# Row copies in place of small transfers for rotated attention queries, and new delays, in a two-layer hybrid trunk

## The chip, the cores and the metric

The kernel runs on one core of one Trainium2 chip. Its time is the device time of one execution in microseconds, as the median of several runs. TensorE (PE in the profile), VectorE (DVE), ScalarE (ACT), GpSimd (POOL) and SyncE (SP) each work through an instruction queue of their own; transfers are issued from the queues of SyncE and ScalarE.

## The reference

The program computes two layers over 1024 tokens of 1024 features. Cut to what the change touches:

```python
def hybrid_layer(x, ...):
    mod = c_act @ w_mod + b_mod                     # shift, scale, gate
    h = rms_norm(x, pre_gain) * (1.0 + scale) + shift
    proj = h @ w_in                                 # columns for three head groups
    aq = apply_rotary(aq.reshape(B, S, ATTN_HEADS, HEAD_DIM), positions, rope_freq)
    ak = apply_rotary(ak.reshape(B, S, ATTN_KV_HEADS, HEAD_DIM), positions, rope_freq)
    a_out = sliding_window_attention(aq, ak, av, sinks) * jax.nn.silu(ag)
    ...
    y = jnp.concatenate([a_out, r_out, g_out], axis=-1) @ w_out
    return x + gate * rms_norm(y, post_gain)

def apply_rotary(x, positions, inv_freq):
    ...
    x1, x2 = jnp.split(x.astype(jnp.float32), 2, axis=-1)
    out = jnp.concatenate([x1 * cos - x2 * sin, x2 * cos + x1 * sin], axis=-1)
```

The attention has 8 query heads of 64 features over 2 key heads, a window of 128 tokens and one learned sink per head. Retention and gated linear attention have 4 heads each and run in chunks.

## The kernel before, in words

Tokens lie in 8 tiles of 128. Weights and activations are split into a high and a low part (`fp32r`, a rounding copy, and the residue), and each product is made in three passes. So each projected tile needs two small jobs per half of its features: a rounding copy on ScalarE (L650) and a subtraction for the residue (L651). The entries `hlo0` and `hlo1` of the table `EN` name the engine of the residue of the first and the second half: GpSimd (G) and VectorE (V). They are used for tiles 2 to 7 of layer 0 and all 8 of layer 1, 14 each. L624 scales a tile by its norm before TensorE transposes it (L176) into PSUM. Weights stream through buffers `st`, are rounded by L145 on ScalarE or L147 on VectorE, and their residues made by L497 on VectorE or GpSimd into `arena`; the output weights are scaled as well (L486, L487).

PSUM has 8 banks: 3 under the name `mm` for the large products, 5 under `aux` for everything else.

The order of TensorE's work is made by a planner in the kernel's text: it keeps a clock of the work issued (`clk`), a list of jobs (generators) and flags. A job yields a delay or a flag to wait for; at points between the wide products (`pump`) the planner runs the jobs that are due. The delays stand in the table `L`, looked up by `lat(key, layer)`; a key with `@1` is for layer 1. The order on the other engines follows from that order and a scheduler's model. No delay is waited for on the chip; they only place the work in the queues.

The attention of a layer goes so. `attn_kv` rotates the keys of a tile on VectorE (`rotary`, L842 to L848), transposes them on TensorE and splits them into `kT` (L858, L859). `attn_rot` is called four times per layer, for the two halves of the tokens (`hf`) and the two head groups (`g`). It loads cosine and sine from `tabS`, makes the projected queries transposed, 128 features by 512 tokens, in two products, and rotates them on VectorE: L890 and L891 multiply, L893 and L894 add. The result in `u[0]`, `u[1]` has its halves of 32 rows in the wrong partitions. So L897 copies `u[j]` to `q[j]` on ScalarE, and four transfers (the entry `qst`, on SyncE, issued in the helper `dma` at L150) then move 32 rows of 512 numbers each, 64 KB, from `u` to other partitions of `q`. After the delay `aq6` a job splits `q` into `mx` (L858 on ScalarE, L859 on VectorE) and sets the flag on which the scores wait, later by `aq2`.

`attn_run` goes through blocks of two tiles: `attn_scores` makes the scores of a tile in 12 small products, into two aux banks; `attn_turn` copies the previous key tile's half (L145, `smx<-aux`, on ScalarE) and the masked half (L957, VectorE), takes the maximum (L959), exponentials (L962), reciprocal (L965) and scales (L966, GpSimd), and after the delay `aq3` transposes the probabilities on TensorE (L176) into an aux bank each, which ScalarE copies out (L145, `t<-aux`). `attn_values` multiplies them by the values (`va`, `vd`) into one more aux bank, copied out by L145 as well.

In the retention part, L1407 loads the values of a chunk back from `vS` (entry `lv`, on SyncE); L1435 makes the gates of the gated linear attention after the chunks that `GGC` names. At the start, `mod_first` makes the first modulation rows, with pieces of the angle tables between its steps (`TAB_N`), and finishes the first half at the step `FIN`.

Of the kernel before, what the change touches and what calls it, by code (L numbers as in the profile page):

```python
# [13 lines left out]
AF = mybir.ActivationFunctionType  # L14
# [5 lines left out]
S = 1024  # L20
# [69 lines left out]
def trunk(ctx: ExitStack, tc: tile.TileContext, ins, cst, out):  # L90
    nc = tc.nc
    V, A, G, T = nc.vector, nc.scalar, nc.gpsimd, nc.tensor
# [16 lines left out]
    def t2(dt=F32):  # L109
        return gp.tile([P, 512], dt, tag="t2", name=nm("t2"), bufs=B2)  # L110
# [13 lines left out]
    def aux(dt=F32):  # L124
        return ps.tile([P, 512], dt, tag="aux", name=nm("aux"), bufs=8 - MMB)
# [14 lines left out]
    def eng(k):  # L140
        return G if EN[k] == "G" else V

    def copy(k, dst, src):
        if EN[k] == "A":
            A.activation(dst, src, AF.Copy)  # L145
        else:
            V.tensor_copy(dst, src)  # L147

    def dma(k, dst, src):
        {"S": nc.sync, "A": A, "P": G}[EN[k]].dma_start(dst, src)  # L150

# [138 lines left out]
    def mod_first(rws, between):  # L290
# [20 lines left out]
        for hh in range(2):  # L311
# [9 lines left out]
            for k in range(KT):  # L321
# [151 lines left out]
    def load(l, name, first=None, kcs=range(KT // 2)):  # L473
# [6 lines left out]
        for kc in kcs:  # L480
# [16 lines left out]
            i = (G if first == 0 and kc in LOG else V if first == 0 else eng(f"wlo{kc}")).tensor_tensor(wt[:, 1, 2 * kc:2 * kc + 2, 0:256], st, f(hi), ALU.subtract)  # L497
            if EN[f"wlo{kc}"] == "G" and first is None:
                after[3] = i
# [106 lines left out]
    def pre(l, t, xt, early=False, soon=False):  # L606
# [9 lines left out]
        with ExitStack() as es:  # L616
# [3 lines left out]
            for j in range(2):  # L620
                if EN[f"xn{j}"] == "A" or early and XA[t][j] == "A" or soon and XA[t][j] == "A":
                    A.activation(xn[j], xt[j], AF.Copy, scale=r)
                else:
                    scaled[t] = V.tensor_scalar(xn[j], xt[j], r, None, ALU.mult)  # L624
        yield 0.5 if early else L["pf1"] if soon else lat("pre1", l)
        if early:
# [252 lines left out]
    def attn_rot(l, hf, g, w_):  # L879


        sn, cs = t2(), t2()
        for s, d in ((0, sn), (1, cs)):
            nc.sync.dma_start(d.rearrange("p (s n) -> p s n", s=2),
                              tabS[2 * hf:2 * hf + 2, :, s, :].rearrange("s p n -> p s n"))
        u, w = [t2(), t2()], [t2(), t2()]
        for c in range(2):
            pm = mm()
            project_T(pm, l, hf, w_, c * P)
            V.tensor_tensor(u[c], pm, cs, ALU.mult)  # L890
            V.tensor_tensor(w[1 - c], pm, sn, ALU.mult)  # L891
            pump()
        V.tensor_tensor(u[0], u[0], w[0], ALU.subtract)  # L893
        V.tensor_tensor(u[1], u[1], w[1], ALU.add)  # L894
        q = w
        for j in range(2):
            A.activation(q[j], u[j], AF.Copy)  # L897
            for r in range(2):
                dst, src = 64 * r + 32 * (1 - j), 64 * r + 32 * j
                dma("qst", q[j][dst:dst + 32], u[1 - j][src:src + 32])  # L900
        mq = mix_tile().rearrange("p a k q -> p (a k q)").rearrange("p (a j n) -> p a j n", a=2, j=2)
        kv[(hf, g)] = mq
        job(split_later(mq, q, ("q", l, hf, g)))
# [438 lines left out]
    def layer(l):  # L1342
# [58 lines left out]
        for p in range(NP_):  # L1401
# [170 lines left out]
B2 = 14  # L1572
B1 = 7
BS, BST, MMB, SMB = 11, 5, 3, 6
EN = {"qst": "S", "smh": "S", "sml": "S", "sm0": "S", "sm1": "S", "lao": "S", "sao": "S", "lmix": "S", "ssg": "S", "lsg": "S", "ssr": "S", "lsr": "A", "lx": "S", "sx": "A", "lw": "S", "lwm": "S", "whi0": "V", "whi1": "A", "whi2": "A", "whi3": "A", "wlo0": "V", "wlo1": "G", "wlo2": "V", "wlo3": "G", "xn0": "V", "xn1": "V", "hlo0": "G", "hlo1": "V", "rot0": "V", "rot1": "V", "rdec": "V", "kslo": "V", "qslo": "V", "vlo": "G", "kT": "A", "qT": "A", "sprev": "A", "pn": "G", "pf0": "A", "aoc": "A", "hng": "V", "mh": "A", "gso": "V", "mg": "V", "mgl": "V", "rT": "A", "rv": "A", "sqh": "A", "sql": "V", "lv": "S", "gv": "A", "gk": "A", "ak0": "V", "ak1": "V", "ak2": "V", "ak3": "V", "kd0": "G", "kd1": "G", "kd2": "G", "kx1": "G", "kx2": "G", "kx3": "V", "kx4": "V", "qb": "G", "stx": "V"}
TURN = ("AV", "AV")
L = {"tt1": 5.86, "tt2": 6.96, "tb1": 28.02, "tb2": 0.32, "pf3": 12.26, "pf1": 6.83, "pf2": 2.88, "mod1": 3.75, "mod2": 2.4, "mod3": 17.58, "mod4": 0.05, "mod5": 0.09, "mod6": 0.05, "pre1": 7.76, "kv1": 15.26, "kv2": 2.17, "aq1": 11.36, "aq7": 4.15, "ag1": 5.72, "aq2": 2.4, "aq6": 7.35, "aq3": 11.38, "aq4": 7.65, "aq5": 2.86, "hn1": 3.34, "hn2": 10.04, "gz1": 9.1, "gz2": 13.49, "gl1": 5.15, "gd3": 15.95, "gc1": 1.82, "gc2": 1.95, "gc3": 0.62, "gc4": 4.49, "gc6": 3.2, "gc5": 4.23, "rc1": 6.33, "rc2": 0.05, "rc3": 1.29, "rc4": 3.27, "fin1": 10.23, "lay1": 0.05, "mod2@1": 2.23, "mod3@1": 15.08, "mod5@1": 2.83, "mod6@1": 3.24, "pre1@1": 10.18, "kv1@1": 4.51, "kv2@1": 0.16, "aq1@1": 6.55, "aq7@1": 7.39, "ag1@1": 8.25, "aq2@1": 2.07, "aq6@1": 9.39, "aq3@1": 11.41, "aq4@1": 6.32, "aq5@1": 1.56, "hn1@1": 4.35, "hn2@1": 9.0, "gz1@1": 6.11, "gz2@1": 8.89, "gl1@1": 20.55, "gd3@1": 15.63, "gc1@1": 2.47, "gc2@1": 4.67, "gc3@1": 0.84, "gc4@1": 0.84, "gc6@1": 1.3, "gc5@1": 0.05, "rc1@1": 5.87, "rc2@1": 2.37, "rc3@1": 2.6, "rc4@1": 5.99, "fin1@1": 6.8, "lay1@1": 0.15, "gc7": 1.43, "gc7@1": 0.05, "tb0": 0.91, "mod7": 1.05, "mod7@1": 1.25}
CHUNK = 7
VDB = 8
VDF = 6  # L1580
TAB_N = (0, 2, 2, 2, 1, 1, 2, 1, 0, 0, 1, 1, 0, 0, 0, 1)
BEGIN = 7
MIXP = (6, 7)
# [47 lines left out]
```

## Time and profile before

| | |
|---|---|
| median of 3 runs | 974.1 us (971.63 to 975.36) |
| profiled execution | 973.24 us |
| its span, first to last instruction | 971.5 us |
| mean granted clock of TensorE | 0.996 |
| TensorE busy | 941.4 us, 97% |
| VectorE busy | 629.3 us, 65% |
| ScalarE busy | 468.0 us, 48% |
| GpSimd busy | 240.5 us, 25% |

The profile is of one execution. The difference between its time and its span, 1.74 us, lies around the first and last instructions. A group of instructions is named by its line, its engine, its operation, and "out<-in" by the names of tiles. A timeline row gives start, duration, engine, line and, in brackets, the idle time before it and whom it waited for. PEld is TensorE's loading of weights, beside its products. The issue of a transfer on an engine's queue (SPq, ACTq) is timed apart from its landing.

### The profile page before, as it was taken

To read this page: it belongs to the slowest core of one execution; us is meant where nothing else is said; L and a number is where in the kernel's file an instruction comes from. 1 tells how busy PE (TensorE), PEld (TensorE's weight loads), DVE (VectorE), ACT (ScalarE), POOL (GpSimd) and SP (SyncE) were. 2 spreads that over 40 slices of the span, in tenths; PEclk is the share of its full clock that TensorE was granted. 3 is DMA by queue.
4 is the path that set the end of the run, shared out by engine and by line. 5 is a ranking of instruction groups with operands and counts; after the bars stand their busy time and mean duration, and the time that the engine had idled before them with its cause. 6 is when DMAs were issued, how large, how long until landed. Compare 5 with 4: busy or idle time off the path is not lost.

```text
span 971.5 us, 15977 instructions
## 1 busy us (share of the span) xinstructions
PE 941.4 (97%) x5645; PEld 769.3 (79%) x5645; DVE 629.3 (65%) x1334; ACT 468.0 (48%) x1149; POOL 240.5 (25%) x302
## 2 busy tenths in 40 slices
PE   5999999999999899999999999999999999999997
PEld 1699888788887677778889888887887777777886
DVE  6876847757785677764677484694667586862332
ACT  2676233454764646623455431434666566761111
POOL 3343001413230324421233110042223033440000
PEclk9999999999999999999999999999999999999999
DMA  9943425513362345687555251262133243555851
GB/s 314 317 133 119 158 72 157 179 34 117 101 199 87 111 141 179 191 273 246 174 173 182 88 180 38 91 195 66 55 99 109 66 131 99 163 174 173 281 218 65
DMA packets 126188, 144.36 MB, mean 149 GB/s; under 512 B 12078, under 2 KB 95896, under 8 KB 126108
## 3 DMA queue, kind: packets, MB, share of 16 engines
q1 hardware_dynamic: 118236, 131.63, 43.8%
q10 hardware_dynamic: 7872, 11.72, 3.4%
q8 instruction: 44, 0.72, 0.3%
q14 instruction: 36, 0.29, 0.1%
HBM read 104.51 MB, written 36.70 MB: 145 GB/s over the span
## 4 chain that ended last, share of the span: by engine, by line
PE 77%; DMA 7%; DVE 5%; ACT 5%; issue 3%; POOL 1%; SPq 0%; ACTq 0%; DVEq 0%; POOLq 0%
PE mm L161 61%; PE aux L161 13%; PE aux L176 3%; DMA st<-in_w_in_dram 1%; DVE arena L497 1%; DMA mx<-mixS 1%; DMA st<-in_w_mod_dram 1%; DMA mixS<-t 1%; DMA t<-t 1%; ACT t L145 1%; DMA xk<-in_x_dram 1%; DMA t<-in_x_dram 1%; DVE t L624 1%; DMA t<-xs 1%; ACT L1016 1%
## 5 line engine op out<-in xcount | busy, mean ns | idle before, releaser
L161 PE MATMUL mm<-arena,arena 128*128 128x512 f32 (+2 forms) x1512 | 314.2, 361 | 0.0
L161 PE MATMUL mm<-arena 128*128 128x512 f32 (+2 forms) x1392 | 286.5, 360 | 0.3 <-ACT arena L698 0.2
L161 PEld LDWEIGHTS mm<-arena,arena 128*128 128x128 f32 x1512 | 246.4, 189 | 43.0 <-issue 2.3
L161 PEld LDWEIGHTS mm<-arena 128*128 128x128 f32 x1392 | 227.6, 189 | 39.3 <-issue 2.0
L161 PE MATMUL mm<-arena,mx 128*128 128x512 f32 (+1 forms) x696 | 158.3, 386 | 0.2 <-DMA mx<-mixS 0.2
L161 PEld LDWEIGHTS mm<-arena,mx 128*128 128x128 f32 x696 | 126.5, 188 | 27.8 <-issue 1.5
L497 POOL TENSOR_TENSOR arena<-st,arena 128x512 fp32r<-128x512 f32 x57 | 84.2, 1484 | 139.2 <-ACT arena L145 80.4
L145 ACT ACTIVATE t<-aux 128x512 f32<-128x512 f32 x64 | 36.8, 590 | 77.4 <-PE aux L176 40.0
L497 DVE TENSOR_TENSOR arena<-st,arena 128x512 fp32r<-128x512 f32 x63 | 65.1, 1048 | 8.5 <-ACT arena L145 5.7
L145 ACT ACTIVATE arena<-st 128x512 fp32r<-128x512 f32 x82 | 48.1, 623 | 42.5 <-PE mm L161 28.4
L1276 ACT ACTIVATE t<-mm 128x512 f32<-128x512 f32 x30 | 18.0, 599 | 95.2 <-PE mm L161 47.8
L962 ACT ACTIVATE smx<-smx,sm 128x129 f32<-128x129 f32 x128 | 50.1, 393 | 20.9 <-DVE sm L959 20.0
L966 POOL TENSOR_TENSOR smx<-smx,sm 128x512 f32<-128x512 f32 x32 | 35.7, 1116 | 90.5 <-DVE sm L965 87.3
L373 DVE SCALAR_TENSOR_TENSOR acc<-st,c_act,acc 128x512 f32<-128x512 f32 x60 | 48.7, 812 | 6.8 <-DMA st<-in_w_mod_dram 6.0
L1277 DVE TENSOR_TENSOR t<-mm,modg 128x512 f32<-128x512 f32 x30 | 20.6, 688 | 43.4 <-ACT t L1276 43.2
L1321 DVE SCALAR_TENSOR_TENSOR t<-t,sm,t 128x512 f32<-128x512 f32 x32 | 25.0, 812 | 34.3 <-DMA t<-xs 18.2
L551 POOL TENSOR_TENSOR sm<-sm,mhalf 128x1 f32<-128x1 f32 x26 | 14.8, 570 | 111.6 <-DVE sm L550 108.7
L176 PE MATMUL aux<-c_ident,t 128*128 128x128 f32 x224 | 33.8, 274 | 6.4 <-DVE t L624 2.7
L176 PEld LDWEIGHTS aux<-c_ident,t 128*128 128x128 f32 x224 | 26.7, 141 | 12.8 <-DVE t L624 3.2
L957 DVE COPY_PREDICATED smx<-c_curmask,aux 128x256 f32<-128x256 int32 x64 | 25.7, 446 | 14.9 <-ACT smx L145 13.7
L359 POOL MEMSET acc<- 128x512 f32 x4 | 2.1, 529 | 124.1 <-PE aux L161 111.3
L1018 DVE TENSOR_TENSOR t<-t,t 128x512 f32<-128x512 f32 x16 | 11.1, 691 | 33.1 <-ACT t L1017 33.1
(223 smaller groups left out, 1349.0 us busy)
## 6 DMA issues: line engine op xcount, KB each, us to landing
st<-in_w_in_dram SPq DMA_DIRECT2D x96, 256.0 KB, 3.2
st<-in_w_mod_dram SPq DMA_DIRECT2D x64, 256.0 KB, 3.7
mixS<-t SPq DMA_DIRECT2D x64, 256.0 KB, 2.6
mx<-mixS SPq DMA_DIRECT2D x28, 512.0 KB, 5.1
st<-in_w_out_dram SPq DMA_DIRECT2D x32, 256.0 KB, 3.2
wm<-in_w_mod_dram SPq DMA_DIRECT2D x12, 512.0 KB, 5.7
t<-in_x_dram SPq DMA_DIRECT2D x24, 256.0 KB, 4.8
t<-tabS SPq DMA_DIRECT2D x16, 256.0 KB, 2.7
```

The lines of the kernel that those rows point to most:

```text
L145: A.activation(dst, src, AF.Copy)
L161: T.matmul(dst, lhsT, rhs, start=start, stop=stop)
L176: T.transpose(dst, src, idn)
L373: V.scalar_tensor_tensor(acc, wt, c_act[:, k:k + 1], acc, ALU.mult, ALU.add)
L497: i = (G if first == 0 and kc in LOG else V if first == 0 else eng(f"wlo{kc}")).tensor_tensor(wt[:, 1, 2 * kc:2 * kc + 2, 0:256], st, f(hi ...
L551: after[2] = G.tensor_tensor(r, r, mhalf[:, :w], ALU.pow)
L957: V.copy_predicated(sv, curmask.unsqueeze(1).to_broadcast((P, 2, P)), pv[:, :, n // P - 1, :])
L962: A.activation(sm[:, h, :], sm[:, h, :], AF.Exp, bias=mx[:, h:h + 1], accum_out=sums[:, h:h + 1])
L966: eng("pn").tensor_tensor(sm[:, :, 0:128], sm[:, :, 0:128], rs.unsqueeze(2).to_broadcast((P, 4, P)), ALU.mult)
L1276: A.activation(yg, pm, AF.Square, accum_out=ss[:, nh:nh + 1])
L1277: V.tensor_tensor(yg, pm, modg[l][:, 512 * nh:512 * nh + 512], ALU.mult)
L1321: V.scalar_tensor_tensor(xt[j], yg[j], r, xt[j], ALU.mult, ALU.add)
```

## The change

The helper `move` takes the place of `dma` for the rows of the queries: by the table `EN` it is a copy on ScalarE or VectorE. Of the four moves of a call the first is on ScalarE (A), the other three on VectorE (V). `hlo0` goes from GpSimd to VectorE, `lv` from SyncE's queue to ScalarE's. 17 delays of `L` get other numbers, some of them far (`aq2` from 2.4 to 1.11, `ag1@1` from 8.25 to 10.22, `gd3` from 15.95 to 17.16), others by hundredths. `TAB_N`, `GGC` and `FIN` each move one piece of work by a step. The tables stand on one line each in the file; here they are cut to the entries that differ most.

```diff
+    def move(k, dst, src):
+        if EN[k] in "SP":
+            dma(k, dst, src)
+        elif EN[k] == "A":
+            A.activation(dst, src, AF.Copy)
+        else:
+            eng(k).tensor_copy(dst, src)
...
             for r in range(2):
                 dst, src = 64 * r + 32 * (1 - j), 64 * r + 32 * j
-                dma("qst", q[j][dst:dst + 32], u[1 - j][src:src + 32])
+                move(f"qst{2 * j + r}", q[j][dst:dst + 32], u[1 - j][src:src + 32])
...
-EN: "qst": "S"
+EN: "qst0": "A", "qst1": "V", "qst2": "V", "qst3": "V"
-EN: "hlo0": "G", "lv": "S"
+EN: "hlo0": "V", "lv": "A"
-L: "aq2": 2.4, "aq3": 11.38, "hn2": 10.04, "gd3": 15.95, "gc6": 3.2, "tb0": 0.91, "mod4": 0.05
+L: "aq2": 1.11, "aq3": 11.35, "hn2": 10.67, "gd3": 17.16, "gc6": 2.54, "tb0": 1.39, "mod4": 0.67
-L: "aq1@1": 6.55, "ag1@1": 8.25, "gz1@1": 6.11, "gz2@1": 8.89, "gc3@1": 0.84
+L: "aq1@1": 6.75, "ag1@1": 10.22, "gz1@1": 5.99, "gz2@1": 8.59, "gc3@1": 0.54
...
-TAB_N = (0, 2, 2, 2, 1, 1, 2, 1, 0, 0, 1, 1, 0, 0, 0, 1)
+TAB_N = (0, 2, 2, 2, 1, 1, 1, 2, 0, 0, 1, 1, 0, 0, 0, 1)
-GGC = ((), (1, 2), (3,), ())
+GGC = ((), (1,), (2, 3), ())
-FIN = 0
+FIN = 1
```

Line numbers after the new helper are 8 higher in the changed kernel (L858 becomes L866). The copies of rows are L153 on ScalarE and L155 on VectorE there.

The numbers also move instructions. Three places, as they stand in the queues. First TensorE in layer 0, from the first block's scores (`kT,mx` into `aux`) to the second's; the second call's queries are being projected there (`arena_356,arena_71`, 24 products for each of two banks). Before:

```order
L161 MATMUL aux_3319<-kT_2168,mx_3210 128x256
L161 MATMUL aux_3332<-t_558_3266,bones 128x512
L161 MATMUL aux_3332<-t_559_3267,bones 128x512
L161 MATMUL mm_3273<-arena_71,arena_356 128x512 x8
L161 MATMUL mm_3398<-arena_356,arena_71 128x512 x24
L161 MATMUL mm_3429<-arena_356,arena_71 128x512 x20
L161 MATMUL aux_3459<-kT_2167,mx_3210 128x256
```

And in the changed kernel:

```order
L169 MATMUL aux_3314<-kT_2168,mx_3210 128x256
L169 MATMUL mm_3263<-arena_71,arena_356 128x512 x4
L169 MATMUL aux_3358<-t_559_3277,bones 128x512
L169 MATMUL aux_3358<-t_560_3278,bones 128x512
L169 MATMUL mm_3263<-arena_71,arena_356 128x512 x8
L169 MATMUL mm_3396<-arena_356,arena_71 128x512 x24
L169 MATMUL mm_3428<-arena_356,arena_71 128x512 x16
L169 MATMUL aux_3454<-kT_2167,mx_3210 128x256
```

The second block's scores come after 16 products of the second bank, not 20; between the two blocks' scores there are 52 large products in both.

Second ScalarE in layer 0, around the third block: `t_582` and its neighbour are the rotated queries of the third call, `mx_3549` their split, `aux_3630` (then `aux_3626`) the bank with the second pair's values, `aux_3661` (then `aux_3657`) the third block's scores. Before:

```order
L897 ACTIVATE t_582_3396<-t_580_3394 128x512
L897 ACTIVATE t_583_3397<-t_581_3395 128x512
L858 ACTIVATE mx_3549<-t_582_3396 128x512
L858 ACTIVATE mx_3549<-t_583_3397 128x512
L145 ACTIVATE arena_356<-st_3734 128x512
L145 ACTIVATE arena_356<-st_3738 128x512
L486 ACTIVATE arena_356<-st_3742,gncol 128x512
L145 ACTIVATE t_620_3637<-aux_3630 128x512
L145 ACTIVATE smx_3657<-aux_3661 128x2x128
```

And in the changed kernel:

```order
L905 ACTIVATE t_582_3395<-t_580_3393 128x512
L905 ACTIVATE t_581_3394<-t_579_3392 128x512
L153 ACTIVATE t_581_3394<-t_580_3393 32x512
L866 ACTIVATE mx_3549<-t_582_3395 128x512
L866 ACTIVATE mx_3549<-t_581_3394 128x512
L145 ACTIVATE arena_356<-st_3734 128x512
L145 ACTIVATE t_620_3633<-aux_3626 128x512
L145 ACTIVATE smx_3653<-aux_3657 128x2x128
```

A row copy stands between L905 and L866, and one of two weight casts (`st_3738`) and the scaled one (`st_3742`) stand no longer ahead of the banks' copies. VectorE at the same place, before:

```order
L859 TENSOR_TENSOR mx_3549<-t_582_3396,mx_3549 128x512
L147 CAST arena_356<-st_3730 128x512
L497 TENSOR_TENSOR arena_356<-st_3730,arena_356 128x512
L859 TENSOR_TENSOR mx_3549<-t_583_3397,mx_3549 128x512
L497 TENSOR_TENSOR arena_356<-st_3738,arena_356 128x512
L487 SCALAR_TENSOR_TENSOR arena_356<-st_3742,gncol,arena_356 128x512
L957 COPY_PREDICATED smx_3640<-c_curmask,aux_3643 128x2x128
```

And in the changed kernel, with the row copies of the same call:

```order
L155 COPY t_582_3395<-t_579_3392 32x512 x2
L155 COPY t_581_3394<-t_580_3393 32x512
L898 TENSOR_TENSOR t_613_3570<-mm_3574,t_612_3567 128x512
L899 TENSOR_TENSOR t_616_3573<-mm_3574,t_611_3566 128x512
L867 TENSOR_TENSOR mx_3549<-t_581_3394,mx_3549 128x512
L867 TENSOR_TENSOR mx_3549<-t_582_3395,mx_3549 128x512
L147 CAST arena_356<-st_3730 128x512
L505 TENSOR_TENSOR arena_356<-st_3730,arena_356 128x512
L965 COPY_PREDICATED smx_3636<-c_curmask,aux_3639 128x2x128
```

The residue of `st_3738` and the scaled one now come after the masked copy of the scores.

Third VectorE in layer 1, where the keys of a tile (`t_1356`) are rotated, before and then in the changed kernel:

```order
L147 CAST arena_356<-st_7835 128x512
L497 TENSOR_TENSOR arena_356<-st_7835,arena_356 128x512
L497 TENSOR_TENSOR arena_356<-st_7843,arena_356 128x512
L847 TENSOR_TENSOR t_1356_7777<-t_1357_7778,t_1358_7779 128x2x32
L848 TENSOR_TENSOR t_1356_7777<-t_1357_7778,t_1358_7779 128x2x32
```

```order
L147 CAST arena_356<-st_7835 128x512
L505 TENSOR_TENSOR arena_356<-st_7835,arena_356 128x512
L855 TENSOR_TENSOR t_1356_7777<-t_1357_7778,t_1358_7779 128x2x32
L856 TENSOR_TENSOR t_1356_7777<-t_1357_7778,t_1358_7779 128x2x32
L938 COPY smx_8228<-sink_434 128x4
L938 COPY smx_8246<-sink_434 128x4
L1202 TENSOR_TENSOR stG<-stC,c_hmask 128x256
L505 TENSOR_TENSOR arena_356<-st_7843,arena_356 128x512
```

The residue of `st_7843` has moved from ahead of the rotation to behind it.

More of the change, by code (lines that the diff above doesn't have):

```diff
@@ L1574 @@
 BS, BST, MMB, SMB = 11, 5, 3, 6
-EN = {"qst": "S", "smh": "S", "sml": "S", "sm0": "S", "sm1": "S", "lao": "S", "sao": "S", "lmix": "S", "ssg": "S", "lsg": "S", "ssr": "S", "lsr": "A", "lx": "S", "sx": "A", "lw": "S", "lwm": "S", "whi0": "V", "whi1": "A", "whi2": "A", "whi3": "A", "wlo0": "V", "wlo1": "G", "wlo2": "V", "wlo3": "G", "xn0": "V", "xn1": "V", "hlo0": "G", "hlo1": "V", "rot0": "V", "rot1": "V", "rdec": "V", "kslo": "V", "qslo": "V", "vlo": "G", "kT": "A", "qT": "A", "sprev": "A", "pn": "G", "pf0": "A", "aoc": "A", "hng": "V", "mh": "A", "gso": "V", "mg": "V", "mgl": "V", "rT": "A", "rv": "A", "sqh": "A", "sql": "V", "lv": "S", "gv": "A", "gk": "A", "ak0": "V", "ak1": "V", "ak2": "V", "ak3": "V", "kd0": "G", "kd1": "G", "kd2": "G", "kx1": "G", "kx2": "G", "kx3": "V", "kx4": "V", "qb": "G", "stx": "V"}
+EN = {"qst0": "A", "qst1": "V", "qst2": "V", "qst3": "V", "smh": "S", "sml": "S", "sm0": "S", "sm1": "S", "lao": "S", "sao": "S", "lmix": "S", "ssg": "S", "lsg": "S", "ssr": "S", "lsr": "A", "lx": "S", "sx": "A", "lw": "S", "lwm": "S", "whi0": "V", "whi1": "A", "whi2": "A", "whi3": "A", "wlo0": "V", "wlo1": "G", "wlo2": "V", "wlo3": "G", "xn0": "V", "xn1": "V", "hlo0": "V", "hlo1": "V", "rot0": "V", "rot1": "V", "rdec": "V", "kslo": "V", "qslo": "V", "vlo": "G", "kT": "A", "qT": "A", "sprev": "A", "pn": "G", "pf0": "A", "aoc": "A", "hng": "V", "mh": "A", "gso": "V", "mg": "V", "mgl": "V", "rT": "A", "rv": "A", "sqh": "A", "sql": "V", "lv": "A", "gv": "A", "gk": "A", "ak0": "V", "ak1": "V", "ak2": "V", "ak3": "V", "kd0": "G", "kd1": "G", "kd2": "G", "kx1": "G", "kx2": "G", "kx3": "V", "kx4": "V", "qb": "G", "stx": "V"}
```

2 lines of the change are left out of this document (1 added, 1 removed).

## The prediction

> **What bounds the kernel now.** I read the page first, for what is short in the whole span.
>
> ```profile
> span 971.5 us, 15977 instructions
> PE 941.4 (97%) x5645; PEld 769.3 (79%) x5645; DVE 629.3 (65%) x1334; ACT 468.0 (48%) x1149; POOL 240.5 (25%) x302
> ```
>
> TensorE is busy in 97% of the span, and the change leaves its work as it is. So at most 971.5 − 941.4 = 30.1 us can be won, only where TensorE waits. The waits of TensorE come next (engine, line, whom it waited for: us in total, times, longest).
>
> ```profile
> PE aux L176 <- DVE smx L957: 4.0, 2, 2.1
> PE aux L176 <- DVE t L624: 2.7, 2, 2.2
> PE aux L176 <- ACT t L145: 1.9, 1, 1.9
> PE aux L176 <- DVE t L848: 1.8, 1, 1.8
> PE aux L161 <- ACT t L1158: 1.2, 2, 0.9
> ```
>
> The windows say where these lie (length, then the busy us and, in brackets, the instructions of PE, PEld, DVE, ACT and POOL; then clock, DMA share, GB/s).
>
> ```profile
> 40.00:60.00 20.00, 19.41 (x157) 18.82 (x157) 15.78 (x35) 15.61 (x44) 10.95 (x14) 1.00 0.71 216
> 60.00:80.00 20.00, 19.47 (x163) 19.20 (x162) 15.26 (x33) 16.93 (x42) 7.06 (x7) 1.00 0.26 77
> 80.00:100.00 20.00, 19.98 (x153) 18.58 (x152) 15.02 (x28) 11.35 (x24) 6.15 (x7) 1.00 0.44 132
> 320.00:340.00 20.00, 16.13 (x97) 12.72 (x98) 14.46 (x26) 12.68 (x36) 7.51 (x7) 1.00 0.35 100
> 340.00:360.00 20.00, 17.94 (x87) 13.74 (x88) 14.58 (x28) 6.88 (x25) 5.18 (x8) 0.91 0.53 157
> 500.00:520.00 20.00, 20.00 (x142) 18.86 (x141) 18.27 (x33) 12.28 (x34) 11.69 (x11) 1.00 0.66 191
> 740.00:760.00 20.00, 17.28 (x114) 14.21 (x113) 12.54 (x28) 12.50 (x24) 4.68 (x5) 1.00 0.26 84
> ```
>
> The holes are in layer 0's attention (320 to 360) and in layer 1 around 745. The timeline of TensorE there:
>
> ```profile
> 322.45 0.63 PE L176 MATMUL aux<-c_ident,smx 128*128 128x128 f32 x4 [1.93 <-DVE smx L957]
> 339.89 0.63 PE L176 MATMUL aux<-c_ident,smx 128*128 128x128 f32 x4 [1.95 <-ACT t L145]
> 342.58 1.08 PE L176 MATMUL aux<-c_ident,smx 128*128 128x128 f32 x4 [2.06 <-DVE smx L957]
> 744.95 0.30 PE L176 MATMUL aux<-c_ident,t 128*128 128x128 f32 x1 [1.83 <-DVE t L848]
> ```
>
> TensorE wants a bank of PSUM for the transposed softmax and the five aux banks are held: by scores until L145 on ScalarE and L957 on VectorE have read them, and by the values' sum until L145 has copied it. Why these readers are late stands in the rows of ScalarE, SyncE's queue and VectorE.
>
> ```profile
> 320.40 0.63 ACT L858 ACTIVATE mx<-t 128x512 fp32r<-128x512 f32 x1 [2.17 <-DMA t<-t]
> 336.46 1.15 ACT L858 ACTIVATE mx<-t 128x512 fp32r<-128x512 f32 x2 [5.79 <-DMA t<-t]
> 337.52 1.13 ACT L145 ACTIVATE arena<-st 128x512 fp32r<-128x512 f32 x2
> 338.56 0.71 ACT L486 ACTIVATE arena<-st,gncol 128x512 fp32r<-128x512 f32 x1
> 339.17 0.58 ACT L145 ACTIVATE t<-aux 128x512 f32<-128x512 f32 x1
> ```
>
> ```profile
> 331.10 4.37 SPq L150 DMA_DIRECT2D t<-t  x4
> ```
>
> ```profile
> 338.80 1.76 DVE L859 TENSOR_TENSOR mx<-t,mx 128x512 fp32r<-128x512 f32 x1
> 340.48 0.94 DVE L497 TENSOR_TENSOR arena<-st,arena 128x512 fp32r<-128x512 f32 x1
> 341.34 0.74 DVE L487 SCALAR_TENSOR_TENSOR arena<-st,gncol,arena 128x512 fp32r<-128x512 f32 x1
> 342.00 0.77 DVE L957 COPY_PREDICATED smx<-c_curmask,aux 128x256 f32<-128x256 int32 x2
> 742.31 1.16 DVE L497 TENSOR_TENSOR arena<-st,arena 128x512 fp32r<-128x512 f32 x1 [1.73 <-ACT arena L145]
> 743.39 1.28 DVE L847 TENSOR_TENSOR t<-t,t 128x64 f32<-128x64 f32 x1
> ```
>
> The rotated queries wait for their row transfers: ScalarE stands 5.79 us before L858, because SyncE spends 4.37 us on issuing four transfers. These queries serve a later block; TensorE doesn't want them yet. But L858, the weights' casts behind it and the bank's copy (339.17) are one queue, and so are L859, L497, L487 and L957. The stalls are the transfers' delay, handed on by queue order.
>
> **The moved rows.** Thirty-two transfers go; 24 copies come on VectorE, 8 on ScalarE. No copy of 32 rows is in the trace; the nearest take 512 elements of each of 128 partitions.
>
> ```profile
> L150 SPq DMA_DIRECT2D t<-t x32: 507/581/2273, 296.6 to 813.0; - x32
> L150 SPq DMA_DIRECT2D t<-vS x16: 319/422/517, 89.9 to 598.0; - x16
> L150 ACTq DMA_DIRECT2D t<-srS x8: 366/372/389, 125.9 to 664.7; - x8
> L147 DVE CAST t<-t x16: 391/422/977, 368.1 to 901.9; 128x512 fp32r<-128x512 f32 x16
> L897 ACT ACTIVATE t<-t x16: 614/632/633, 295.9 to 810.8; 128x512 f32<-128x512 f32 x16
> ```
>
> VectorE gets 24 × 0.42 = 10.1 us (9.4 to 23.4 by the ends of the CAST's row), ScalarE 8 × 0.63 = 5.0 us. I take the medians. A call's rows are then there 3 × 0.42 = 1.3 us after the sums, instead of the four issues' 4.37 us and a landing. The windows from 320 to 360 leave VectorE 40 − 29.04 = 10.96 us free; two calls need 2.5 of it. So the copies lie beside TensorE's products, and L858 and L859 run before the scores end instead of across them. What is late next is the bank's own turnover, L957's 0.77/2 = 0.39 and a copy before it that is no longer than 0.58: about 1.0 us, of which some lies under the remaining scores. I leave 0.9 of the three stalls: 1.93 + 1.95 + 2.06 − 0.9 = 5.0 us won. If the DVE cover is gone (each copy at 0.98), a call costs 2.9 us, still less than the transfers.
>
> Against this change speaks a model in the Trainium skill (VectorE: DVE Perf Modes, "Two Vector instructions with no wait between them"): a VectorE instruction whose operand starts in another group of 32 partitions than the one before starts only when all earlier ones have finished. Rows above start 0.08 us before their forerunner's end (340.48 + 0.94 against 341.34), so by it four starts a call would lose 0.3 us, 0.6 in the two calls here, and the sum would win 0.6 less; no row of before has such a copy.
>
> **The delays.** The new delays move TensorE's order by four to twelve products at a time. In the second block the scores come after 16 instead of 20 products of their projection, in the third after 20 instead of 24. The price of one product:
>
> ```profile
> 921.14 38.84 PE mm L161 x168
> ```
>
> That is 38.84/168 = 0.23 us, so four are 0.9 us. The distance from the first block's scores to the second's stays 52 products, so readers get no less time. On ScalarE two weight casts and L486 (1.13/2 + 0.71 = 1.3 us) now stand behind the bank's copy in the third block; on VectorE L497 and L487 (1.7 us) stand behind L957. These orders go the same way as the copies. In layer 1, VectorE's L497 of 742.31, which waited 1.73 us for a cast, stood ahead of the key's rotation L847; in the new order it stands behind. L847 began at 743.39, more than a microsecond late, and the stall of 1.83 should go: 1.8 us won.
>
> **hlo0 on VectorE.** Fourteen residues leave GpSimd.
>
> ```profile
> L651 POOL TENSOR_TENSOR arena<-t,arena x14: 1287/1297/1746, 46.6 to 539.3; 128x512 fp32r<-128x512 f32 x14
> L651 DVE TENSOR_TENSOR arena<-t,arena x14: 677/988/1812, 49.9 to 539.8; 128x512 fp32r<-128x512 f32 x14
> ```
>
> VectorE gets 14 × 0.99 = 13.8 us (9.5 to 25.4). Six fall into 40 to 100 us, where it is free for 60 − 46.06 = 13.9 us and needs 5.9 (at worst 10.9); eight into the stretch to 540, where TensorE is 20.00 of 20 busy even while VectorE is at 18.27, so it has work in stock. I cost it at nothing, with 0 to 2 us for the 40-to-100 stretch, where TensorE has already waited 2.7 us for VectorE's L624. It could win a little too, a residue being 0.3 us earlier; not over 0.5 in all.
>
> The Trainium skill (SBUF — State Buffer, "Who interferes with whom") says that a VectorE instruction with two SBUF inputs is blocked while a GpSimd one that reads SBUF runs. The row's spread, 677 to 1812, agrees, though it does not name the cause; were all fourteen so blocked, the sum would carry 25.4 us on VectorE instead of 13.8, and a kernel that shows them all would take 974.1 − 6.8 + 25.4 = 992.7.
>
> **The small edits.** Sixteen loads t<-vS leave SyncE (16 × 0.42) for ScalarE's queue, 16 × 0.37 = 6.0 us there. Ahead of the first use ScalarE is idle for long stretches:
>
> ```profile
> 113.49 0.60 ACT L1066 ACTIVATE t<-aux 128x512 f32<-128x512 f32 x1 [8.67 <-PE aux L161]
> 585.85 0.60 ACT L145 ACTIVATE t<-aux 128x512 f32<-128x512 f32 x1 [9.24 <-PE aux L176]
> ```
>
> So they cost nothing there; without that cover, a load waiting for its buffer would hold ScalarE's later copies. FIN, TAB_N and GGC each move one piece of work by a step beside products; at zero. For everything that the reordering disturbs elsewhere, I put in +0.5 us, between −1 and +3 (the row of waits for L848 and L1158, 1.8 + 1.2, shows what one or two unlucky orders cost).
>
> **The sum.** 5.0 + 1.8 − 0.5 = 6.3 us won. The profiled execution took 973.24 us, 1.74 more than its span, and becomes 966.9. It lies 0.9 us under the median of the runs, so for the median I forecast 974.1 − 6.3 = 967.8. About 0.5%, or 4.9 us, is what a measurement of this kernel can tell from no change, so this is a narrow "faster".
>
> **Rivals.**
> *The stalls stay, the cause changes.* The third block's ScalarE and VectorE queues stay long: the new copies (2.5 us on VectorE) and L858/L859 are still queued ahead of L957, and five banks are still five. For it: three of four stalls name a bank's reader, none a transfer. Against it: L858 waited 5.79 us and nothing before it did. Then only layer 1's 1.8 us go, and the time is 974.1 − 1.8 = 972.3; with the 3 us of new stalls, 975.3.
>
> *Slower: the residue delays the next tile.* In both layers each moved L651 stands in VectorE's queue before the next tile's scaling L624, whose transposes TensorE awaits. For it: L624 is already a wait of 2.7 us. Against it: VectorE is free for a quarter of that stretch. If all of it shows, 974.1 − 6.8 + 13.8 = 981.1. Slower than before from 6.8/14 = 0.49 us exposed per residue; measurably so from (6.8 + 4.9)/14 = 0.84.
>
> *More is won.* The waits for L624 (2.7) and L1158 (1.2) go as well, since both engines' queues are drained earlier: 967.8 − 3.9 = 963.9, with the disturbance at its low end 962.4. Nothing in the rows ties them to the transfers.
>
> **How the numbers follow.** My forecast 0.56, the stalls stay 0.28, slower 0.08, more won 0.08. That makes faster 0.64, same 0.28, slower 0.08. The forecast's own range is 965.4 (nothing left of the three stalls, the disturbance at −1) to 969.2 (the disturbance at +1.9; a larger one I count with the staying stalls, as no change). The range that should hold 8 in 10 goes to 974.5, into the case of staying stalls, and down to 962.8.
>
> **What would show it.** Right: no wait of ScalarE before L866 (now L858) for a transfer; TensorE above 18.5 busy in 320 to 340 and 19 in 340 to 360; no wait for L856 (now L848) near 740; the 32-row copies at about 0.42. Wrong: waits of L184 for L965 or L145 of the same size at the same blocks (first rival); waits of L184 for L632, or a TensorE below 19.4 between 40 and 100 (second). If the new stalls lie between 130 and 300, the disturbance was mis-sized.

## The result and the profile after

The changed kernel takes 963.58 us as the median of four runs (961.89 to 964.30), against 974.73 for the kernel before in the same comparison (971.63 to 980.84). The ratio is 0.9875, 95% interval 0.9826 to 0.9925. Later comparisons had more runs of the kernel before: medians of 972.88 (27 runs), 972.77 (19) and 972.87 (9). A second set of the changed kernel gave 963.91 and a ratio of 0.9898 (0.9855 to 0.9940). One of its four executions took 1873.51 us, for a reason that nothing here shows; it counts in that median and not in the ratio. So the gain is about 9 us, some 1%. I had forecast 6.3 us.

The page of the changed kernel begins so:

```profile
span 960.2 us, 15949 instructions
PE 940.1 (98%) x5645; PEld 770.2 (80%) x5645; DVE 636.0 (66%) x1372; ACT 474.3 (49%) x1157; POOL 222.6 (23%) x288
```

TensorE's work is what it was (941.4 us before); what went is waiting. The waits of TensorE, in the order of the view and cut (whom it waited for, us in total, times, longest); the longest, 6.0 us for L422 at the start, was 6.2 before:

```profile
...
PE aux L184 <- DVE t L632: 2.2, 1, 2.2
PE aux L184 <- DVE smx L965: 1.5, 3, 0.8
...
PE aux L169 <- ACT t L1166: 1.1, 1, 1.1
```

The waits on masked copies and on L145 at the attention's banks were 4.0 and 1.9 us in all and are now 1.5. The wait for the key's rotation (then L848) is in no row any more. The windows of the same two stretches of layer 0, and of layer 1 around 750, show the same, with DVE the third and the granted clock the third number from the end:

```profile
320.00:340.00 20.00, 19.46 (x116) 15.61 (x115) 18.54 (x30) 12.91 (x37) 10.88 (x10) 1.00 0.37 119
340.00:360.00 20.00, 19.84 (x115) 15.65 (x115) 16.25 (x35) 11.57 (x39) 4.85 (x6) 1.00 0.43 132
740.00:760.00 20.00, 18.79 (x117) 15.34 (x116) 12.48 (x24) 12.91 (x23) 0.79 (x2) 1.00 0.24 66
```

TensorE stands at 19.46 where it had 16.13, and the clock of the second window is 1.00, where it had 0.91. VectorE, at 18.54 of 20, is now close to full. The timeline of TensorE there:

```profile
317.20 0.63 PE L184 MATMUL aux<-c_ident,smx 128*128 128x128 f32 x4 [0.78 <-DVE smx L965]
333.86 0.63 PE L184 MATMUL aux<-c_ident,smx 128*128 128x128 f32 x4 [0.54 <-DVE smx L965]
351.32 1.06 PE L184 MATMUL aux<-c_ident,smx 128*128 128x128 f32 x8 [0.16 <-DVE smx L965]
```

Three waits of 1.93 + 1.95 + 2.06 = 5.94 us have become 1.48. VectorE's chain at the second block shows why the first of them is not zero:

```profile
311.56 0.68 DVE L902 TENSOR_TENSOR t<-t,t 128x512 f32<-128x512 f32 x1
312.16 0.68 DVE L1031 TENSOR_TENSOR t<-t,t 128x512 fp32r<-128x512 f32 x1
312.87 1.30 DVE L155 COPY t<-t 32x512 f32<-32x512 f32 x3
314.21 0.69 DVE L898 TENSOR_TENSOR t<-mm,t 128x512 f32<-128x512 f32 x1
314.81 0.68 DVE L899 TENSOR_TENSOR t<-mm,t 128x512 f32<-128x512 f32 x1
315.41 1.28 DVE L867 TENSOR_TENSOR mx<-t,mx 128x512 fp32r<-128x512 f32 x2
316.61 0.77 DVE L965 COPY_PREDICATED smx<-c_curmask,aux 128x256 f32<-128x256 int32 x2
```

From the rotation's sum to the masked copy VectorE has no gap, and TensorE's transposes at 317.20 wait for the first of the two masked copies in the last row. The row copies lie in that chain: 1.30 us for three. All 24 copies on VectorE and the eight on ScalarE, by line (shortest, median and longest in ns):

```profile
L155 DVE COPY t<-t x24: 414/422/1408, 295.6 to 802.3; 32x512 f32<-32x512 f32 x24
```

```profile
L153 ACT ACTIVATE t<-t x8: 630/632/635, 295.9 to 800.6; 32x512 f32<-32x512 f32 x8
```

In the median a copy of 32 rows takes what one of 128 rows took: 0.42 and 0.63 us, the two prices of the prediction. Seven of VectorE's 24 took longer, 0.46 to 1.41 us, each beside an instruction of GpSimd, so that the 24 are 13.3 us and not 10.1.

### The profile page after: what moved, and what is told of

The parts are those of the page before. It is cut to its first block, busy times and chain, and to the rows that moved or that the text cites. A ratio compares the mean times of both kernels' runs of the same rounds, so it can differ in the third digit from the quotient of the medians.

```text
span 960.2 us, 15949 instructions
## 1 busy us (share of the span) xinstructions
PE 940.1 (98%) x5645; PEld 770.2 (80%) x5645; DVE 636.0 (66%) x1372; ACT 474.3 (49%) x1157; POOL 222.6 (23%) x288
## 4 chain that ended last, share of the span: by engine, by line
PE 89%; ACT 3%; issue 3%; DVE 3%; DMA 1%; POOL 1%; ACTq 0%; DVEq 0%; SPq 0%; POOLq 0%
PE mm L169 70%; PE aux L169 14%; PE aux L184 4%; DMA xk<-in_x_dram 1%; DMA c_freq<-cst_freq_dram 0%; ACT L1024 0%; DVE arena L505 0%; ACT mx L1160 0%; ACT smx L970 0%; ACT t L145 0%; DVE t L1028 0%; DVE t L1026 0%; DMA t<-tabS 0%; ACT L1025 0%; ACT mx L1159 0%
## 5 line engine op out<-in xcount | busy, mean ns | idle before, releaser
L505 POOL TENSOR_TENSOR arena<-st,arena 128x512 fp32r<-128x512 f32 x57 | 85.6, 1507 | 159.4 <-ACT arena L145 105.7
L145 ACT ACTIVATE t<-aux 128x512 f32<-128x512 f32 x64 | 37.1, 590 | 83.9 <-PE aux L184 39.9
L505 DVE TENSOR_TENSOR arena<-st,arena 128x512 fp32r<-128x512 f32 x63 | 64.6, 1039 | 7.7 <-ACT arena L145 4.0
L145 ACT ACTIVATE arena<-st 128x512 fp32r<-128x512 f32 x82 | 48.5, 623 | 33.6 <-PE mm L169 17.3
L974 POOL TENSOR_TENSOR smx<-smx,sm 128x512 f32<-128x512 f32 x32 | 35.5, 1108 | 82.4 <-DVE sm L973 78.6
L381 DVE SCALAR_TENSOR_TENSOR acc<-st,c_act,acc 128x512 f32<-128x512 f32 x60 | 45.4, 757 | 13.6 <-DMA st<-in_w_mod_dram 12.7
L184 PEld LDWEIGHTS aux<-c_ident,t 128*128 128x128 f32 x224 | 27.3, 143 | 10.1 <-DVE t L632 2.6
L850 DVE TENSOR_TENSOR t<-mm,sincos 128x128 f32<-128x128 f32 (+2 forms) x36 | 16.2, 449 | 24.0 <-ACT t L145 13.0
```

The costliest lines, as they stand in the source:

```text
L184: T.transpose(dst, src, idn)
L381: V.scalar_tensor_tensor(acc, wt, c_act[:, k:k + 1], acc, ALU.mult, ALU.add)
L850: V.tensor_tensor(a4, s4, cs.unsqueeze(1).unsqueeze(1).to_broadcast((P, nh, 2, 32)), ALU.mult)
L974: eng("pn").tensor_tensor(sm[:, :, 0:128], sm[:, :, 0:128], rs.unsqueeze(2).to_broadcast((P, 4, P)), ALU.mult)
```

## The experiments

**The row copies alone.** All tables and queues as before.

```diff
-EN: "hlo0": "V", "lv": "A"
+EN: "hlo0": "G", "lv": "S"
-L, TAB_N, GGC, FIN: of the changed kernel
+L, TAB_N, GGC, FIN: of the kernel before
```

> The kernel before with the row copies alone (A, V, V, V), all tables and queues as before. Theory 1 (the transfers' delay is the stall): the waits of TensorE near 322, 340 and 343, 5.94 us together, fall below 2, the granted clock between 340 and 350 stays at 1.00 instead of 0.83 (about 1.7 us), and the time falls by 4 to 7 us; the layer-1 wait of 1.83 stays. Theory 2 (queue order set by the delays is the stall): at least 4 of the 5.94 us stay, and the time moves by less than 2.5 us.

Measured: 972.29 us, ratio 0.9996 (0.9975 to 1.0017): no gain that the runs can tell from none. The timeline of TensorE has one attention wait left, and it is larger:

```profile
324.96 1.09 PE L184 MATMUL aux<-c_ident,smx 128*128 128x128 f32 x4 [4.33 <-DVE smx L965]
```

The two waits of the third block (4.01 us) are gone, as theory 1 had it; the second block's grew from 1.93 to 4.33. VectorE and GpSimd ahead of it:

```profile
321.04 2.36 DVE L867 TENSOR_TENSOR mx<-t,mx 128x512 fp32r<-128x512 f32 x2
323.32 0.41 DVE L147 CAST arena<-st 128x512 fp32r<-128x512 f32 x1
323.77 0.69 DVE L505 TENSOR_TENSOR arena<-st,arena 128x512 fp32r<-128x512 f32 x1
324.38 0.78 DVE L965 COPY_PREDICATED smx<-c_curmask,aux 128x256 f32<-128x256 int32 x2
```

```profile
321.06 1.78 POOL L505 TENSOR_TENSOR arena<-st,arena 128x512 fp32r<-128x512 f32 x1 [2.42 <-ACT arena L145]
```

GpSimd's L505 runs across the pair L867, which takes 2.36 us here and 1.28 in the changed kernel. Behind that pair a weight's cast and residue stand ahead of the masked copy. The three row copies are slower as well, 1.94 us against 1.30; the first of them runs beside GpSimd's L974 (317.60 to 318.64):

```profile
317.86 1.94 DVE L155 COPY t<-t 32x512 f32<-32x512 f32 x3 [0.34 <-ACT t L905]
```

And the clock falls during the wait and stays low behind it (windows of 2 us, clock third from the end):

```profile
322.00:324.00 2.00, 0.00 (x0) 0.00 (x0) 1.97 (x3) 0.08 (x1) 0.84 (x1) 0.68 0.01 2
324.00:326.00 2.00, 1.04 (x5) 1.07 (x6) 1.97 (x5) 0.09 (x1) 0.00 (x0) 0.50 0.51 164
326.00:328.00 2.00, 2.00 (x7) 1.52 (x6) 0.89 (x5) 2.00 (x8) 0.55 (x1) 0.50 0.98 315
328.00:330.00 2.00, 2.00 (x7) 1.62 (x6) 2.00 (x5) 1.78 (x7) 0.83 (x2) 0.61 0.12 43
```

Neither theory holds alone. By its numbers the second comes out (4.33 of the 5.94 us stay, and the time hardly moves), but not at its places: the transfers were the third block's stall, and with the old order the second block's gets worse.

**The delays and steps alone.**

```diff
-EN: "qst0": "A", "qst1": "V", "qst2": "V", "qst3": "V", "hlo0": "V", "lv": "A"
+EN: "qst0": "S", "qst1": "S", "qst2": "S", "qst3": "S", "hlo0": "G", "lv": "S"
```

> The kernel before with the new delays and steps alone; rows by transfers, residues on GpSimd, value loads on SyncE. Theory 1: the layer-0 attention waits stay within 2 us of 5.94, only the layer-1 wait of 1.83 goes, and the time falls by 1 to 3 us. Theory 2: the layer-0 waits fall to 2 or less and the time falls by 6 us or more. A third theory, that the delays were set for the copies and hurt without them: the waits in layer 0 grow over 7 us.

Measured: 968.20 us, ratio 0.9961 (0.9942 to 0.9979). The attention's waits are 2.27 + 1.03 + 0.17 = 3.47 us, between what the two theories allow, and the clock is at 0.50 behind the first.

```profile
321.14 0.63 PE L184 MATMUL aux<-c_ident,smx 128*128 128x128 f32 x4 [2.27 <-DVE smx L965]
339.85 0.63 PE L184 MATMUL aux<-c_ident,smx 128*128 128x128 f32 x4 [1.03 <-DVE smx L965]
```

```profile
318.06 0.63 ACT L866 ACTIVATE mx<-t 128x512 fp32r<-128x512 f32 x1 [2.72 <-DMA t<-t]
```

Here it is the transfer again that the chain waits for, 2.72 us at the second block. So the delays by themselves took three quarters of the third block's waits (4.01 to 1.03), and the transfers hold up the second's.

**The changed kernel without the row copies.**

```diff
-EN: "qst0": "A", "qst1": "V", "qst2": "V", "qst3": "V"
+EN: "qst0": "S", "qst1": "S", "qst2": "S", "qst3": "S"
```

> The changed kernel with the four moves of a call as transfers on SyncE again. Theory 1: the layer-0 attention waits come back, 4 us or more over the changed kernel's 1.48, with a lower granted clock behind them; the start (to 100 us) and the stretch from 130 to 200 stay as in the changed kernel, 2.8 us ahead of the kernel before. Theory 2: the waits stay below 3 us and the time within 1.5 us of the changed kernel's.

Measured: 966.49 us, ratio 0.9934 (0.9914 to 0.9953). The waits are 2.27, 1.12 and 0.17 us, again with a dip of the clock. They come back by 2.1 us, not by the 4 of theory 1, and the time moves by more than theory 2 allows: the copies are worth about 2.7 us (966.49 against 963.58 and 963.91) when the delays are there.

**The residue back on GpSimd.**

```diff
-EN: "hlo0": "V"
+EN: "hlo0": "G"
```

> The changed kernel with the first half's residue on GpSimd again. If the residues' move won the unforeseen time at the start (0.57 and 0.53 us of waits between 40 and 80, and 0.25 at 38), these waits come back, 0.8 us or more later at 100 us; if it was the delays or steps, they stay away and the time is within 0.5 us of the changed kernel's. My prediction's price, nothing either way, is the second.

Measured: 963.72 us, ratio 0.9913 (0.9885 to 0.9941), as the changed kernel. The waits near 39, 46 and 70 us are back, and so they were in all four kernels of this set, whatever the change; this is settled below.

**The changed kernel once more.** The same program.

> The changed kernel once more, for a second profile. If the waits near 39, 46 and 70 us (0.25, 0.57 and 0.53 in the kernel before, none in the changed kernel's profile, all there in the four runs so far) went by the change, they are absent again. If they are a matter of one execution's start, some of them are back, and 0.8 us or more of the profile's 11.35 us was chance. The attention's waits come out within 0.1 us of 0.78, 0.54 and 0.16 either way.

Measured: 963.91 us (ratio 0.9898, 0.9855 to 0.9940); the profiled execution took 964.27, 2.38 us more than the first one.

```profile
46.41 0.65 PE L184 MATMUL aux<-c_ident,t 128*128 128x128 f32 x4 [0.57 <-DVE t L632]
70.49 0.66 PE L184 MATMUL aux<-c_ident,t 128*128 128x128 f32 x4 [0.44 <-DVE t L654]
```

The waits at the start are back, so the first profile's lack of them was that execution's chance. The attention's came out at 0.77, 0.54 and 0.16. Profile against profile, the change wins 973.24 − 964.27 = 9.0 us, which agrees with the medians of the longer comparisons.

**The row copies and one delay.**

```diff
-L: "aq2": 2.4
+L: "aq2": 1.11
```

(on the kernel with the row copies alone)

> The kernel with the row copies alone, and of all new numbers only aq2 = 1.11. In the queue order L147 and L505 no longer stand ahead of the second block's masked copies. Theory A (these two are what the copies alone lacked): the wait of 4.33 falls by 1.06 us or more, the clock's dip behind it shrinks, and the time falls by 2 us or more against the row copies alone. Theory B (the copies come too late against the scores, whatever stands behind them, since scores come four products earlier with this aq2): the wait stays above 3.5 us and the time does not move by more than 1 us.

Measured: 967.30 us, ratio 0.9948 (0.9926 to 0.9970), 5.0 us less than the copies alone (972.29).

```profile
320.40 0.63 PE L184 MATMUL aux<-c_ident,smx 128*128 128x128 f32 x4 [1.80 <-DVE smx L965]
337.24 0.63 PE L184 MATMUL aux<-c_ident,smx 128*128 128x128 f32 x4 [0.79 <-DVE smx L965]
```

```profile
318.62 1.28 DVE L867 TENSOR_TENSOR mx<-t,mx 128x512 fp32r<-128x512 f32 x2
319.82 0.78 DVE L965 COPY_PREDICATED smx<-c_curmask,aux 128x256 f32<-128x256 int32 x2
```

The wait fell by 4.33 − 1.80 = 2.53 us. Cast and residue no longer stand between (323.32 to 324.38, 1.06 us); and since ScalarE's cast for GpSimd's L505 moved behind too, that L505 starts only at 324.58 in this run, and the pair L867 takes 1.28 instead of 2.36 (1.08 us). Those two make 2.14 of the 2.53. The clock stays at 1.00 from 320 to 330, where the copies alone lost (1.04 + 2.00) × 0.50 + 2.00 × 0.39 = 2.3 us of TensorE's work by the windows above. With the waits (4.33 against 1.80 + 0.79, 1.7 us) that is 4.0 of the 5.0 us; the rest lies outside the attention and within what the runs scatter. (In layer 1 two new waits, 0.50 and 1.19 us near 652, stand against the key rotation's 1.61, which is gone.) Theory A holds. The row copies still take 1.94 us here, beside GpSimd's L974; the changed kernel's wait is a further 1.02 us shorter, and the 0.64 us of these copies is part of that.

**The changed kernel with that delay as before.**

```diff
-L: "aq2": 1.11
+L: "aq2": 2.4
```

> The changed kernel with aq2 = 2.4 again, all else as changed. If this one delay is what makes the row copies pay (they alone left a wait of 4.33 us, with it 1.80), L147 and L505 stand ahead of the second block's masked copies again, the wait of 0.78 grows to 3 us or more with a dip of the granted clock to about 0.5 behind it, and the time is 3 to 5 us longer than the changed kernel's. If the other delays had made it unnecessary, the wait stays below 1.8, without a dip, and the time within 1 us.

Measured: 967.93 us, ratio 0.9941 (0.9921 to 0.9961), 4.0 to 4.4 us more than the changed kernel's two medians.

```profile
322.16 1.09 PE L184 MATMUL aux<-c_ident,smx 128*128 128x128 f32 x4 [4.32 <-DVE smx L965]
```

```profile
322.00:324.00 2.00, 1.84 (x7) 1.68 (x8) 1.85 (x7) 0.89 (x4) 0.00 (x0) 0.50 0.63 200
324.00:326.00 2.00, 2.00 (x6) 1.55 (x5) 1.01 (x2) 2.00 (x9) 0.64 (x1) 0.50 0.68 223
```

The wait is the one of the copies alone, with the same dip. Its pieces are back too: the row copies at 1.94 us, the pair below beside GpSimd's L505, and the cast (320.51) and the residue (320.96) ahead of the masked copy (321.57).

```profile
318.24 2.35 DVE L867 TENSOR_TENSOR mx<-t,mx 128x512 fp32r<-128x512 f32 x2
```

**Each row copy twice.**

```diff
                 move(f"qst{2 * j + r}", q[j][dst:dst + 32], u[1 - j][src:src + 32])
+                move(f"qst{2 * j + r}", q[j][dst:dst + 32], u[1 - j][src:src + 32])
```

> The changed kernel with each row copy made twice, so 24 more copies on VectorE and 8 more on ScalarE; nothing left out. If the copies lie beside other work everywhere, as I costed them, the time moves by less than 0.5 us. If their cover ends at the second block, where VectorE goes from the copies straight to the masked copies, the wait of 0.78 there grows by 1.0 to 1.5 us, to about 2, with a dip of the granted clock behind it, and the rest stays: 1.5 to 3 us slower. If VectorE is short everywhere, it is 5 us or more.

Measured: 968.91 us, ratio 0.9960 (0.9941 to 0.9980), 5 us more than the changed kernel.

```profile
320.97 0.77 PE L184 MATMUL aux<-c_ident,smx 128*128 128x128 f32 x4 [3.08 <-DVE smx L966]
339.13 0.63 PE L184 MATMUL aux<-c_ident,smx 128*128 128x128 f32 x4 [0.48 <-DVE smx L966]
```

```profile
322.00:324.00 2.00, 2.00 (x6) 1.61 (x5) 1.75 (x6) 2.00 (x8) 0.55 (x1) 0.50 0.00 0
```

The place is the one named, the second block, and the third doesn't change (0.48). The size is larger than I expected, 2.30 us more of wait and a dip behind it, where the three extra copies are 1.3 us. The trace shows most of the rest: the extra copies of the first call put the first block's masked copies 1.77 us behind the start of its scores (303.11 against 301.34), where the changed kernel has 0.92 (300.80 against 299.88), and the 0.85 us between them is still there when L902 starts at the second block. I had also expected the rest to stay, and it did not: layer 1 has a new wait of 0.55 us for a masked copy at 798.43.

**The three steps as before.**

```diff
-TAB_N = (0, 2, 2, 2, 1, 1, 1, 2, 0, 0, 1, 1, 0, 0, 0, 1)
+TAB_N = (0, 2, 2, 2, 1, 1, 2, 1, 0, 0, 1, 1, 0, 0, 0, 1)
-GGC = ((), (1,), (2, 3), ())
+GGC = ((), (1, 2), (3,), ())
-FIN = 1
+FIN = 0
```

> The changed kernel with TAB_N, GGC and FIN as before, the delays new. If the moved gate product (GGC) ended the wait of 1.26 us near 192, it is back and the stretch from 140 to 200 is 1 to 2 us longer; if the delays (gd3, gc6, hn2) did, it stays away and the time is within 0.5 us of the changed kernel's. By my prediction, which put these steps at zero, the second.

Measured: 964.51 us, ratio 0.9908 (0.9872 to 0.9943); 0.6 to 0.9 us over the changed kernel's medians, which the runs can't tell from nothing.

```profile
191.06 0.72 PE L169 MATMUL aux<-t 64*128 64x128 f32 x8 [1.27 <-ACT t L145]
```

But the trace can: the wait near 191 is back, and the one of 0.44 near 158, which the changed kernel has instead, is not there. So the steps win that wait, 0.8 us net by the trace; which of the three does was not tried, though only the gate product of GGC stands in that stretch.

**The value loads back on SyncE.**

```diff
-EN: "lv": "A"
+EN: "lv": "S"
```

> The changed kernel with the sixteen value loads on SyncE's queue again. By my price, nothing: the waits of TensorE stay as in the changed kernel, 0.55 near 137 and 0.44 near 159 among them, and the time is within 0.5 us of it. If the move had won the stretch from 140 to 200, the wait of 1.26 near 191 comes back.

Measured: 963.78 us, ratio 0.9899 (0.9866 to 0.9931): nothing. The waits near 137 and 159 are 0.54 and 0.45 us, and there is none near 191.

**One row copy more on ScalarE.**

```diff
-EN: "qst3": "V"
+EN: "qst3": "A"
```

> The changed kernel with the fourth row copy on ScalarE too (A, V, V, A): one copy of 0.43 us less on VectorE's chain ahead of the second block's masked copies, one of 0.63 more on ScalarE, whose copies of the scores wait 0.31 for TensorE there. If VectorE's chain is the last, the wait of 0.78 falls to about 0.4 and the time by up to 0.5 us, not to be told from none by the runs. If ScalarE's becomes the last, the wait grows over 0.9.

Measured: 962.70 us (962.31 to 963.65), ratio 0.9890 (0.9862 to 0.9917), the lowest median here; the intervals do not tell it from the changed kernel.

```profile
318.33 0.63 PE L184 MATMUL aux<-c_ident,smx 128*128 128x128 f32 x4 [0.45 <-DVE smx L965]
```

The second block's wait fell from 0.78 to 0.45, by about one copy's time, and the third's (0.54) went altogether. VectorE's chain was the last there.

## Why the prediction was right or wrong

The forecast was 967.8. The measured 963.58 is 4.2 us below it: outside the forecast's own range (965.4 to 969.2), inside the wider one meant to hold 8 in 10 (962.8 to 974.5). The direction was right. In the mechanism, what failed is the step on the delays; in the size, the clock and the sign of the disturbance. The third rival's 963.9 is nearly the measured time, but by chance: the waits that it counted on, 2.7 us for L624 and 1.2 for L1158, are still 2.8 and 1.1 in the second profile of the changed kernel. Step by step:

**What bounds it: right.** The gain is TensorE's waiting, at the places named.

**"The stalls are the transfers' delay, handed on by queue order": right for the third block, short for the second.** With the transfers gone and all else as before, the third block's 4.01 us went and the second block's wait grew by 2.40. The prediction shows VectorE's queue ahead of the masked copies for the third block alone, and puts the copies down as lying "beside TensorE's products". With the new order that is nearly so; with the old one VectorE is the last in line at the second block, and the kernel takes 972.29 us. That happens to be the time of my first rival (972.3), which came about in another way: it kept the stalls of the third block, and the run has the second's.

**The delays, "these orders go the same way as the copies": the step that failed.** I took them for helpers, with no term of their own in the attention and +0.5 us of loss elsewhere. Alone, all delays and steps win 0.39% and the copies nothing that can be told from none; together they win 1%. With the copies, aq2 by itself is 5.0 us (and 4.0 to 4.4 when it is taken out of the changed kernel), because it takes three pieces of weight work out of the way at the second block: a cast and a residue on VectorE, and GpSimd's residue beside L867. I had priced such pieces at the third block, where the copies alone end the waits as well, and not at the second, where they decide. The kernel before has the same two there, ahead of its masked copies:

```profile
319.93 0.42 DVE L147 CAST arena<-st 128x512 fp32r<-128x512 f32 x1
320.38 0.69 DVE L497 TENSOR_TENSOR arena<-st,arena 128x512 fp32r<-128x512 f32 x1
321.85 0.45 DVE L957 COPY_PREDICATED smx<-c_curmask,aux 128x256 f32<-128x256 int32 x1
```

And elsewhere the reordering won 1.0 us instead of losing 0.5. The copies with aq2 alone stand at 967.30 us; the further 3.4 us to 963.91 come from the other delays and steps, of which only the steps were tried apart (0.6 to 0.9 us). A slip beside it: the prediction says that two weight casts moved behind the bank's copy in the third block; its sum counts one (1.13/2), and one is what moved.

**A term left out: the granted clock.** The row of 340 to 360 in the kernel before showed 0.91, and I quoted it without a price. The windows of 2 us there:

```profile
342.00:344.00 2.00, 1.42 (x6) 1.36 (x7) 1.97 (x8) 0.41 (x3) 0.00 (x0) 0.58 0.72 174
344.00:346.00 2.00, 2.00 (x7) 1.57 (x6) 1.16 (x2) 2.00 (x8) 1.14 (x2) 0.57 0.81 299
```

TensorE worked for 1.42 and 2.00 us of them, so 1.42 × 0.42 + 2.00 × 0.43 = 1.5 us of its time were lost behind two waits, and are gone with them. (The 1.7 in the expectation of the row copies alone also counts the part of the first window in which TensorE waited.) The two figures are means over 2 us; at a clock of 0.50 they stand for (0.42 + 0.43) × 2 / 0.50 = 3.4 us at half clock. The Trainium skill (TensorE: Matmul & The Clock Gate, "Part 1: The HAM clock gate") says that an idle TensorE falls to half its clock and needs a few microseconds of work to get it back. The traces agree on the half (0.50) and on the few microseconds (3.4 here, and 6.8 with the copies alone); they differ on how long it must idle, which the page puts at about 3.4 us: a single wait of 2.27 us was enough.

**The sum, term by term,** against the kernel before, from the waits of the second profile of the changed kernel: attention 5.94 − 1.47 = 4.5 (forecast 5.0, near in size, but laid to the copies, which alone took 5.94 − 4.33 = 1.6); clock 1.5 (forecast none); layer 1 with the waits 0.35 + 0.46 + 1.83 + 0.90 against 0.47 + 1.13, 1.9 (forecast 1.8, right); the stretch from 130 to 200 with 0.55 + 0.15 + 1.26 against 0.55 + 0.44, 1.0 (forecast a loss of 0.5). These make 8.9 us, where profile against profile measures 9.0. Part of that agreement is chance, since the sum leaves out the start, where the second profile lies 0.86 us behind the kernel before (the wait near 137 ends at 137.96 against 137.10); about as much was won outside the waits listed. Against the forecast's 6.3 the clock is 1.5 of the difference and the disturbance, with the other sign, 1.5; the attention's waits gave 0.5 less. The rest of the 4.2 us is the starting point: I counted from 974.1, the median of three runs, where the longer comparisons have 972.8 to 972.9.

**hlo0 at nothing: right in time, wrong in its working.** I put 13.8 us on VectorE. The rows of the changed kernel, and of the one with the residue back on GpSimd:

```profile
L659 DVE TENSOR_TENSOR arena<-t,arena x28: 671/684/700, 48.3 to 530.5; 128x512 fp32r<-128x512 f32 x28
```

```profile
L659 POOL TENSOR_TENSOR arena<-t,arena x14: 1272/1295/1500, 46.7 to 531.4; 128x512 fp32r<-128x512 f32 x14
L659 DVE TENSOR_TENSOR arena<-t,arena x14: 677/798/1818, 50.6 to 531.9; 128x512 fp32r<-128x512 f32 x14
```

With both halves on VectorE none takes over 0.70 us; all 28 are about 19.2 us (28 × 0.684), where 14 took 15.2 before by the group's mean of 1084 ns. The load grew by 4 us. In the kernel before, the eight of VectorE's fourteen residues that began while the other half was running on GpSimd took 0.88 to 1.81 us, and the other six 0.68 to 0.69. The rule of the Trainium skill that I weighed (SBUF — State Buffer, "Who interferes with whom") agrees with that, and the same rule fits the pair L867, 2.36 us under GpSimd's L505 and 1.28 without. I had used it for the wrong side: the move took the contention away.

**The held copies: no more than the small price I set.** L1031 ends at 312.16 + 0.68 = 312.84 and the first row copy starts at 312.87, with no overlap, while L902 (to 312.24) and L1031 overlap by 0.08. So the model of the Trainium skill (VectorE: DVE Perf Modes, "Two Vector instructions with no wait between them") agrees, at about 0.1 us a time.

**lv at nothing, layer 1's key rotation: right,** by their runs and rows. The slower rival did not come about: the waits for L632 are 2.8 us in the second profile, where L624's were 2.7.

## What to carry to other kernels

When a change brings both new instructions and a new order, cost the order as a term of its own: name what stands ahead of the critical reader in each of the two orders and what it takes, on every engine that shares a port or a queue with it. A stall of TensorE is priced with the granted clock of the windows behind it. And a gap that only one profile shows, at the start above all, is looked for in a second execution before it is counted.

## What the runs showed of the hardware

The clock of TensorE fell to 0.50 with single waits of 2.27, 3.08, 4.32 and 4.33 us, and with two of 1.95 and 2.06 that had one group of work between them; it stayed at 1.00 after single waits of 1.80 and 1.93. Counted from the windows as above, it was low for 3.4 us in the kernel before and for 6.8 with the copies alone, (0.32 + 0.50 + 0.50 + 0.39) × 2 / 0.50. In the kernel before that cost 1.5 us on top of the waits. No run changed a wait's length by itself, so whether its length alone decides, and where between 1.93 and 2.27 us a limit would lie, is open.

VectorE's instructions were slower beside GpSimd. In the kernel before a residue of 128x512 took 0.68 to 0.69 us, and 0.88 to 1.81 when it began while the other half was running there. Three row copies took 1.94 us instead of 1.30 where the first ran beside GpSimd's L974.

A copy that moves 32 rows to other partitions took 0.42 us on VectorE and 0.63 on ScalarE, the median time of 128 rows with the same 512 elements each; other lengths were not tried.
